# Reordering the start of an adaLN decoder block: evictions placed behind the next casts, the first modulation as wide products, and looser background sums

## The chip, the cores and the metric

The kernel runs on one core of a Trainium2 chip. The metric is the device time of one execution in microseconds, the median over several executions. The engines of the core are named as in the profile: PE multiplies matrices (PEld is its loading of weights), DVE and ACT work on vectors, POOL does a few side jobs here, and SP issues nearly all transfers from the chip's memory. PE writes into eight accumulator banks (PSUM). A bank is usable again when ACT or DVE has copied its content away, which is called an eviction below. Each engine works through its instructions in the order in which they were placed, so an instruction that waits holds up those behind it on the same engine.

## The reference

One decoder layer on 256 tokens of width 2048, all in float32:

```python
mod = jax.nn.silu(c) @ w_ada[l] + b_ada[l]
shift1, scale1, gate1, shift2, scale2, gate2 = jnp.split(mod[:, None, :], N_MOD, axis=-1)
h = rms_norm(x, norm1_gain[l]) * (1 + scale1) + shift1
x = x + gate1 * mixing_sublayer(h, ...)
h = rms_norm(x, norm2_gain[l]) * (1 + scale2) + shift2
x = x + gate2 * swiglu(h, w_ffn_in[l], w_ffn_out[l])
```

The mixing sublayer projects `h` with `w_in` (13 column blocks of 512 for queries, keys and values, then more for gates), runs three branches (stick-breaking attention, dilated window attention, gated linear attention), gates and sums them, and projects with `w_out`. The conditioning vector `c` gives six modulation vectors of 2048 through the matrix `w_ada` of 2048 x 12288, some 100 MB.

## The kernel before, in words

**Products.** All large products are made from three float32r products (`mm3`, lines 180 to 182): the high part of the activations with the high part of the weights, with the low part of the weights, and the low part of the activations with the high part of the weights. Each weight tile of two k-chunks (128 x 1024, 512 KB) is loaded by SP into a `raw` tile (line 161), rounded by ACT into `whi` (line 172, a cast), and DVE subtracts to get `wlo` (line 173). `whi` and `wlo` have four buffers each. The width of 2048 is cut into 16 chunks of 128; the tokens into two halves, so each column block needs two accumulator banks.

**The first chunks** (`first_chunks`). The input projection starts before all of `h` exists. `x` and the rows of `w_ada` for chunk 0 are loaded first. PE sums the squares of `x` (line 553), DVE and ACT make the root (`root_of`), and the modulation of chunk 0 is a sum over 16 row tiles: ten of them as products on PE with one moving column each (line 724, two per row tile), six of them weighted and added on DVE (line 738) and reduced by one more pair of products. `keep_warm` (line 704) puts products without use between them. Then `make_h` gives `h` for chunk 0, and `start_block` multiplies it with 13 column blocks (line 682), each of 6 products, in the order 1, 2, 3, 4, 9, 10, 11, 12, 0, 5, 6, 7, 8. The results are evicted to the tiles `A0` to `A12` (`evict`, line 630), except those of blocks 5 to 8, which stay in the banks until chunks 1 and 2 are added. Blocks 3, 4, 11, 12, 6 and 7 use the four `misc` banks, the others the four `acc` banks, so block 12 takes over the banks of block 4, and block 10 those of block 2. Meanwhile the modulations of chunks 1 and 2 are made on DVE: `columns` and `chunk_macs` call `column_mac` (line 433), a multiply with a running sum over 1024 columns, four per chunk. Inside `first_chunks` the context `in_order` pins PE, ACT and DVE to the order in which the code is written.

**The visits.** Then 26 visits (`proj_block` from the loop over `visits`) add chunks 1 to 10 to the column blocks, a few chunks at a time, while `ada_chunks` makes the modulation of the next chunks. A visit copies `A[b]` back into two banks (line 618), loads and casts its weights, multiplies, and evicts to `A[b]` again (line 630). Visits take the `acc` and the `misc` banks in turn. After the visits, 13 more blocks (`LAST`) finish the projection while the attention begins.

**Background.** The other four modulation segments are made in small steps between products (`tick` calls the generator `background`). `ada_segment_steps` loads half a row of `w_ada` into a ring of tiles, and `mac` issues the DVE sum. 128 such sums are spread over the stretch from 228 us to 948 us.

**Order.** Outside `in_order`, a scheduler places instructions by priority (`prio` raises it) and readiness, from its own estimate of times. `tc.issue_after(ins)` adds an ordering edge behind `ins`, but only for those instructions of the block that run on the engine of `ins`; others get no edge. `state["split"]` is the newest subtraction of line 173 or 234, on DVE. `state["mm"]` is the newest product of line 182, on PE. `state["cast"]` is the newest cast of line 172, on ACT.

**Constants.** The stick-breaking branch needs three small constant tiles that are loaded behind the visits: `k_low` (line 871, cast by ACT at line 872), `k_bias` (line 873, added by DVE at line 952), and `k_dist`.

Of the kernel before, what the change touches and what calls it, by code (L numbers as in the profile page):

```python
# [17 lines left out]
P = 128  # L18
# [68 lines left out]
def trunk(ctx: ExitStack, tc: tile.TileContext, I, out):  # L87
# [408 lines left out]
    ring = {"tags": ("AR0", "AR1"), "n": 0}  # L496
# [7 lines left out]
    def mac():  # L504
        v, seg, j, half, raw, done = macs.pop(0)
        with tc.issue_after(state["split"].ins):
            column_mac(v, seg, j, half, raw)
        if done is not None:
            after.append(done)

    def ada_segment_steps(v, seg, done):


        for j in range(KC):
            for half in range(2):

                while len(macs) >= len(ring["tags"]) - ring.get("spare", len(ring["tags"]) > 3):
                    mac()
                raw = araw([P, HALF])
                with prio(), tc.issue_after(state["loads_after"]) if "loads_after" in state else nullcontext():  # L520
                    load_column(raw, seg, j, half)
# [109 lines left out]

    def first_chunks():
# [9 lines left out]
        def load_two(k, b, single=False):  # L642
            raw = raws[k, b] = wp.tile([P, 2, NB], F32, tag="raw", name=nm("raw"))
# [6 lines left out]
        def load_one(k, b):  # L650
            raw = raws[k, b] = wp.tile([P, 2, NB], F32, tag="raw", name=nm("raw"))
# [32 lines left out]
        def x_in(j, a, b):  # L684
            nc.sync.dma_start(xT[j][:, a:b], I["x_t"][:, 4 * j + a : 4 * j + b, :])

        def mods_in(j, a, b):
            nc.sync.dma_start(rows[j][:, a:b], I["ada_0"][:, 4 * j + a : 4 * j + b, :])

# [6 lines left out]
        for b in (3, 9, 11):  # L696
            load_two(0, b)
        load_mods(1, (0, 1))

# [6 lines left out]
        with in_order():  # L706
            csil = silu_of_c()
            near1 = small([P, 1])
            nc.vector.tensor_scalar(near1, vec[:, BADA + SEG_SCALE1 * KC : BADA + SEG_SCALE1 * KC + 1], 1.0, None, op0=ALU.add)
# [8 lines left out]
            mods = [acc_bank([P, 1]) for _ in range(2)]  # L718
            part = S("T6", [P, 2 * P])

            def by_pe(lhs, k, stop=False):
                for i in range(2):
                    c = slice(i * P, (i + 1) * P)
                    nc.tensor.matmul(
                        mods[i], lhs[:, c], eps_c[:, 2:3] if k is None else csil[:, k : k + 1], start=k == 0, stop=stop
                    )

            def on_pe(*ks):
                for k in ks:
                    by_pe(rows[k // 4][:, k % 4, :], k)  # L730
# [16 lines left out]
            on_dve(2, 3)  # L747
            on_pe(0, 1)
            r = state["root"] = root_of(sums)
            keep_warm(WARM[5])  # L750
            on_pe(4, 5)
            on_dve(6, 7)
# [1019 lines left out]
```

## Time and profile before

| | us |
|---|---|
| median of 3 runs | 1593.93 (1589.18 to 1599.44) |
| the profiled execution, its own time | 1592.44 |
| span in its profile | 1590.7 |
| PE busy in the span | 1560.7 |
| DVE busy | 1372.6 |
| ACT busy | 917.4 |

The profile's page lists busy time per engine, the span in 40 slices, and the costliest groups of instructions. Busy PE is not PE at its peak: products overlap, so the better measure is the number of products in a stretch. A table of stretches gives for each the length, and per engine the busy time with the number of instructions in brackets, then the granted PE clock (1.00 is full), the share of the transfer engines, and GB/s. A line of the timeline gives start, duration, engine, line, operation, output and inputs, count, and in square brackets how long the engine had been idle before and what ended that.

### The profile page before, as it was taken

To read this page: it belongs to the slowest core of one execution; us is meant where nothing else is said; L and a number is where in the kernel's file an instruction comes from. 1 tells how busy PE (TensorE), PEld (TensorE's weight loads), DVE (VectorE), ACT (ScalarE), POOL (GpSimd) and SP (SyncE) were. 2 spreads that over 40 slices of the span, in tenths; PEclk is the share of its full clock that TensorE was granted. 3 is DMA by queue.
4 is the path that set the end of the run, shared out by engine and by line. 5 is a ranking of instruction groups with operands and counts; after the bars stand their busy time and mean duration, and the time that the engine had idled before them with its cause. 6 is when DMAs were issued, how large, how long until landed. Compare 5 with 4: busy or idle time off the path is not lost.

```text
span 1590.7 us, 20098 instructions
## 1 busy us (share of the span) xinstructions
PE 1560.7 (98%) x7082; PEld 1283.0 (81%) x7082; DVE 1372.6 (86%) x1838; ACT 917.4 (58%) x1292; POOL 5.0 (0%) x11
## 2 busy tenths in 40 slices
PE   9999999999999999999998999999999999999998
PEld 8687778788887878888876888888888888888887
DVE  7888877788898999987886878999999999789886
ACT  6786677775765655344434745555655555455553
POOL 0000000000000000000000000000000000000000
PEclk9999999999999999999999999999999999999999
DMA  9998968767777777989898776666566566656664
GB/s 330 399 351 316 349 225 299 242 222 221 242 270 264 261 272 240 309 288 339 305 320 292 264 241 204 194 213 208 186 191 220 185 199 225 199 186 192 231 206 138
DMA packets 113780, 399.20 MB, mean 251 GB/s; under 512 B 12528, under 2 KB 13424, under 8 KB 113680
## 3 DMA queue, kind: packets, MB, share of 16 engines
q1 hardware_dynamic: 113104, 395.84, 73.4%
q0 software_dynamic: 576, 2.10, 0.3%
q8 instruction: 55, 0.90, 0.2%
q14 instruction: 45, 0.37, 0.1%
HBM read 393.69 MB, written 4.19 MB: 250 GB/s over the span
## 4 chain that ended last, share of the span: by engine, by line
PE 58%; DMA 4%; DVE 3%; issue 1%; ACT 1%; SPq 0%; ACTq 0%; DVEq 0%
PE acc L181 12%; PE acc L182 12%; PE acc L180 12%; PE misc L181 7%; PE misc L182 7%; PE misc L180 7%; DMA raw<-w_out 3%; DVE wlo L173 1%; ACT whi L172 1%; PE misc L1407 0%; DMA A<-x_blocks 0%; DMA T<-w_in 0%; DMA KD<-ada_t 0%; DVE wlo L234 0%; PE acc L1407 0%
## 5 line engine op out<-in xcount | busy, mean ns | idle before, releaser
L181 PE MATMUL acc<-wlo,H 128*128 128x512 f32 (+1 forms) x856 | 335.6, 392 | 5.4 <-DVE wlo L173 3.1
L180 PE MATMUL acc<-whi,H 128*128 128x512 f32 (+1 forms) x856 | 333.4, 393 | 4.3 <-ACT whi L172 4.3
L182 PE MATMUL acc<-whi,H 128*128 128x512 f32 (+1 forms) x856 | 334.3, 391 | 0.0
L172 ACT CAST whi<-raw 128x1024 fp32r<-128x1024 f32 x204 | 209.8, 1035 | 202.7 <-PE acc L182 95.4
L173 DVE TENSOR_TENSOR wlo<-raw,whi 128x1024 fp32r<-128x1024 f32 x204 | 242.1, 1197 | 91.8 <-ACT whi L172 91.2
L181 PEld LDWEIGHTS acc<-wlo,H 128*128 128x128 f32 x856 | 161.2, 188 | 42.3 <-DVE wlo L173 7.1
L180 PEld LDWEIGHTS acc<-whi,H 128*128 128x128 f32 x856 | 160.8, 188 | 38.6 <-ACT whi L172 5.6
L182 PEld LDWEIGHTS acc<-whi,H 128*128 128x128 f32 x856 | 161.1, 188 | 32.7 <-DVE H L598 0.2
L248 ACT CAST whi<-raw 128x1024 fp32r<-128x1024 f32 (+1 forms) x133 | 128.1, 977 | 80.1 <-PE acc L182 32.2
L234 DVE TENSOR_TENSOR wlo<-raw,whi 128x1024 fp32r<-128x1024 f32 (+1 forms) x133 | 147.8, 1127 | 17.2 <-ACT whi L248 16.1
L181 PE MATMUL misc<-wlo,H 128*128 128x512 f32 x285 | 111.5, 391 | 1.1 <-DVE wlo L173 1.0
L182 PE MATMUL misc<-whi,H 128*128 128x512 f32 x285 | 110.4, 388 | 0.0
L180 PE MATMUL misc<-whi,H 128*128 128x512 f32 x285 | 108.9, 388 | 1.1 <-ACT whi L172 1.1
L181 PE MATMUL acc<-wlo,A 128*128 128x512 f32 x210 | 82.6, 393 | 4.3 <-DVE wlo L173 4.2
L182 PE MATMUL acc<-whi,A 128*128 128x512 f32 x221 | 86.3, 391 | 0.0
L180 PE MATMUL acc<-whi,A 128*128 128x512 f32 x210 | 82.4, 392 | 2.4 <-ACT whi L172 2.4
L181 PEld LDWEIGHTS misc<-wlo,H 128*128 128x128 f32 x285 | 53.5, 188 | 15.1 <-DVE wlo L173 4.4
L180 PEld LDWEIGHTS misc<-whi,H 128*128 128x128 f32 x285 | 53.4, 188 | 12.5 <-ACT whi L172 1.5
L182 PEld LDWEIGHTS misc<-whi,H 128*128 128x128 f32 x285 | 53.5, 188 | 10.8
L234 DVE TENSOR_TENSOR A<-raw,A 128x1024 fp32r<-128x1024 f32 (+2 forms) x58 | 54.3, 943 | 2.7 <-ACT A L248 2.1
L630 ACT COPY A<-acc 128x512 f32<-128x512 f32 x66 | 37.6, 592 | 28.5 <-PE acc L182 25.6
L433 DVE CUSTOM_DVE_ANT_0 AR<-AR,ada,vec 128x1024 f32<-128x1024 f32 x36 | 46.1, 1279 | 7.9 <-DMA AR<-ada_t 7.9
(725 smaller groups left out, 3265.0 us busy)
## 6 DMA issues: line engine op xcount, KB each, us to landing
raw<-w_in SPq DMA_DIRECT2D x143, 512.0 KB, 5.6
raw<-w_ffn_in SPq DMA_DIRECT2D x137, 512.0 KB, 4.5
raw<-w_ffn_out SPq DMA_DIRECT2D x74, 512.0 KB, 4.4
AR<-ada_t SPq DMA_DIRECT2D x71, 512.0 KB, 5.5
X<-w_in SPq DMA_DIRECT2D x34, 512.0 KB, 5.3
raw<-w_out SPq DMA_DIRECT2D x32, 512.0 KB, 7.4
OS<-ada_t SPq DMA_DIRECT2D x29, 512.0 KB, 7.3
KD<-ada_t SPq DMA_DIRECT2D x22, 512.0 KB, 6.2
```

The lines of the kernel that those rows point to most:

```text
L172: state["cast"] = nc.scalar.copy(hi[:, :n, :], raw[:, :n, :])
L173: state["split"] = nc.vector.tensor_tensor(lo[:, :n, :], raw[:, :n, :], hi[:, :n, :].bitcast(F32), op=ALU.subtract)
L180: nc.tensor.matmul(ps, lh, rh, start=start, stop=False, skip_group_check=seeded)
L181: nc.tensor.matmul(ps, lh, rl, start=False, stop=False, skip_group_check=seeded)
L182: state["mm"] = nc.tensor.matmul(ps, ll, rh, start=False, stop=stop, skip_group_check=seeded)
L234: done = nc.vector.tensor_tensor(dst, x, y, op=ALU.subtract)
L248: nc.scalar.copy(hi[:, :n, :], src)
L433: return nc.vector.tensor_tensor_reduce(out=raw, in0=raw, in1=cB[:, half * HALF : (half + 1) * HALF], scale=1.0, scalar=part if half else ...
L630: nc.scalar.copy(A[b][:, t, :], pss[t])
```

## The change

There are five parts.

1. **Visits.** A new function `visit` replaces `proj_block` in the loop over `visits`. It leaves the finished banks in a list `pending` and evicts up to two of them behind the last cast of the next visit. At the end of `first_chunks` only block 5 is evicted at once; 6, 8 and 7 go into the list.
2. **Chunk 0's modulation.** The stationary operand is now one column of silu(c) repeated 128 times, the moving operand a row tile of 256 columns, so that every partition of one bank holds all 256 sums, and one product per row tile replaces two. DVE picks the diagonal with a multiply-and-sum against the identity (for the scale, the identity times the norm gain). PE takes row tiles 0, 1, 4, 5 and 8 to 13, DVE 2, 3, 6, 7, 14 and 15. Two calls of `keep_warm` go.
3. **Order of the first chunks.** Loads are issued earlier into tiles that are free by then, casts stand one eviction earlier, and `make_h` for chunk 1 stands ahead of the cast of block 7 and the eviction of block 4, where it stood behind the eviction of block 11.
4. **Early constant.** The load of `k_low` gets a raised priority.
5. **Background.** The ring of the first stage has three tiles in place of two, of which one stays spare; `mac` and its load name the newest product in `issue_after` in place of the newest subtraction.

```diff
--- before.py
+++ after.py
@@ -493,7 +493,7 @@
                         make_h(k)
                     yield
 
-    ring = {"tags": ("AR0", "AR1"), "n": 0}
+    ring = {"tags": ("AR0", "AR1", "OD"), "n": 0}
 
     def araw(shape, dtype=F32):
         ring["n"] += 1
@@ -503,7 +503,7 @@
 
     def mac():
         v, seg, j, half, raw, done = macs.pop(0)
-        with tc.issue_after(state["split"].ins):
+        with tc.issue_after(state["mm"].ins):
             column_mac(v, seg, j, half, raw)
         if done is not None:
             after.append(done)
@@ -514,11 +514,12 @@
         for j in range(KC):
             for half in range(2):
 
-                while len(macs) >= len(ring["tags"]) - ring.get("spare", len(ring["tags"]) > 3):
+                while len(macs) >= len(ring["tags"]) - ring.get("spare", len(ring["tags"]) > 2):
                     mac()
                 raw = araw([P, HALF])
-                with prio(), tc.issue_after(state["loads_after"]) if "loads_after" in state else nullcontext():
-                    load_column(raw, seg, j, half)
+                with tc.issue_after(state["loads_after"]) if "loads_after" in state else nullcontext():
+                    with prio(), tc.issue_after(state["mm"].ins):
+                        load_column(raw, seg, j, half)
                 macs.append((v, seg, j, half, raw, done if (j, half) == (KC - 1, 1) else None))
                 yield
 
@@ -629,6 +630,20 @@
             for t in range(NT):
                 nc.scalar.copy(A[b][:, t, :], pss[t])
 
+    pending = []
+
+    def visit(k0, k1, b, bank, carry):
+        pss = [bank([P, NB]) for _ in range(NT)]
+        with prio():
+            for t in range(NT):
+                nc.scalar.copy(pss[t], A[b][:, t, :])
+        w = load_weights(w_in, k0, k1, b)
+        with tc.issue_after(state["cast"].ins):
+            for _ in range(min(2, len(pending))):
+                evict(*pending.pop(0))
+        block(pss, h_at, w_in, k0, k1, b, w=w, go_on=True, more=carry, seeded=True)
+        (carried if carry else pending).append(pss if carry else (b, pss))
+
     def first_chunks():
 
 
@@ -639,16 +654,19 @@
             for i in which:
                 load_column(rows[4 * k + i], (SEG_SCALE1, SEG_SHIFT1)[i // 2], k, i % 2)
 
-        def load_two(k, b, single=False):
-            raw = raws[k, b] = wp.tile([P, 2, NB], F32, tag="raw", name=nm("raw"))
+        def raw_at(tag):
+            return S(tag, [P, 2, NB]) if tag else wp.tile([P, 2, NB], F32, tag="raw", name=nm("raw"))
+
+        def load_two(k, b, single=False, tag=None):
+            raw = raws[k, b] = raw_at(tag)
             for n in range(2) if single else (slice(0, 2),):
                 if single:
                     nc.sync.dma_start(raw[:, n, :], w_in[b + n, :, k, :])
                 else:
                     nc.sync.dma_start(raw, w_in[b : b + 2, :, k, :].rearrange("b p c -> p b c"))
 
-        def load_one(k, b):
-            raw = raws[k, b] = wp.tile([P, 2, NB], F32, tag="raw", name=nm("raw"))
+        def load_one(k, b, tag):
+            raw = raws[k, b] = raw_at(tag)
             nc.sync.dma_start(raw[:, 0, :], w_in[b, :, k, :])
 
         def cast_one(k, b):
@@ -681,21 +699,17 @@
                 for t in range(NT):
                     nc.tensor.matmul(pss[t], h_at(k, t)[l], r, start=start and i == 0, stop=stop and i == 2)
 
...
         nc.sync.dma_start(vec, I["k_vec"])
         for j in range(4):
             nc.sync.dma_start(xT[j], I["x_t"][:, 4 * j : 4 * j + 4, :])
         for j, a, b in ((0, 0, 4), (1, 0, 4), (2, 0, 4), (3, 0, 2), (3, 2, 4)):
             nc.sync.dma_start(rows[j][:, a:b], I["ada_0"][:, 4 * j + a : 4 * j + b, :])
         load_two(0, 1, True)
-        for b in (3, 9, 11):
-            load_two(0, b)
+        load_two(0, 3)
         load_mods(1, (0, 1))
+        load_two(0, 9)
+        load_mods(1, (2, 3))
+        load_two(0, 11)
 
         spare = acc_bank()
 
@@ -705,8 +719,12 @@
 
         with in_order():
             csil = silu_of_c()
-            near1 = small([P, 1])
-            nc.vector.tensor_scalar(near1, vec[:, BADA + SEG_SCALE1 * KC : BADA + SEG_SCALE1 * KC + 1], 1.0, None, op0=ALU.add)
+            gain = vec[:, ROW_N1 : ROW_N1 + 1]
+            o = [BADA + seg * KC for seg in (SEG_SCALE1, SEG_SHIFT1)]
+            near = small([P, 1])
+            nc.vector.scalar_tensor_tensor(near, vec[:, o[0] : o[0] + 1], 1.0, gain, op0=ALU.add, op1=ALU.mult)
+            diag = scr([P, P])
+            nc.vector.tensor_scalar(diag, ident, gain, None, op0=ALU.mult)
             keep_warm(WARM[0])
             turned = spread(csil, [cB[:, q * NB : (q + 1) * NB] for q in range(4)], "KC", True)
             next(turned)
@@ -715,19 +733,15 @@
             for _ in turned:
                 pass
             sums = acc_bank([P, T])
-            mods = [acc_bank([P, 1]) for _ in range(2)]
+            mods = acc_bank([P, 2 * P])
             part = S("T6", [P, 2 * P])
 
-            def by_pe(lhs, k, stop=False):
-                for i in range(2):
-                    c = slice(i * P, (i + 1) * P)
-                    nc.tensor.matmul(
-                        mods[i], lhs[:, c], eps_c[:, 2:3] if k is None else csil[:, k : k + 1], start=k == 0, stop=stop
-                    )
+            def by_pe(lhs, rhs, k, stop=False):
+                nc.tensor.matmul(mods, lhs, rhs, start=k == 0, stop=stop)
 
             def on_pe(*ks):
                 for k in ks:
-                    by_pe(rows[k // 4][:, k % 4, :], k)
+                    by_pe(csil[:, k : k + 1].to_broadcast([P, P]), rows[k // 4][:, k % 4, :], k)
 
             def on_dve(*ks):
                 for k in ks:
@@ -744,27 +758,33 @@
             squares(2, "AR0", sums)
             keep_warm(WARM[4])
             squares(3, "AR1", sums)
-            on_dve(2, 3)
+            on_dve(2, 3, 6, 7)
             on_pe(0, 1)
             r = state["root"] = root_of(sums)
-            keep_warm(WARM[5])
-            on_pe(4, 5)
-            on_dve(6, 7)
-            keep_warm(WARM[6])
-            on_pe(8, 9)
+            on_pe(4, 5, 8, 9, 10, 11)
+            on_dve(14, 15)
+            on_pe(12, 13)
+            by_pe(ones, part, None, True)
             for dst, ps in state["spreads"]:
                 nc.scalar.copy(dst, ps)
-            on_dve(10, 11)
-            on_pe(12, 13)
-            by_pe(part, None)
-            on_pe(14)
-            by_pe(rows[3][:, 3, :], 15, True)
+            load_one(0, 0, "X1")
+            load_two(0, 5, tag="X2")
+            load_two(0, 7, tag="AR0")
+            load_two(1, 5, tag="AR1")
+            load_two(1, 7, tag="KC")
+            rows.extend(S(tag, [P, HALF]) for tag in FIRST_TAGS[:4])
+            load_mods(2, range(4))
+            load_two(2, 5, tag="KD")
+            load_two(2, 7)
             cast_two(0, 1, True)
             lows(0, 1)
-            sh, sc = (mod1[seg][:, 1, 0:1] for seg in (SEG_SHIFT1, SEG_SCALE1))
-            nc.vector.scalar_tensor_tensor(sc, mods[0], near1, vec[:, ROW_N1 : ROW_N1 + 1], op0=ALU.add, op1=ALU.mult)
-            o = BADA + SEG_SHIFT1 * KC
-            nc.vector.tensor_tensor(sh, mods[1], vec[:, o : o + 1], op=ALU.add)
+            for i, seg in enumerate((SEG_SCALE1, SEG_SHIFT1)):
+                col = slice(i * P, (i + 1) * P)
+                nc.vector.tensor_tensor_reduce(
+                    out=part[:, col], in0=mods[:, col], in1=ident if i else diag, scale=1.0,
+                    scalar=vec[:, o[1] : o[1] + 1] if i else near, op0=ALU.mult, op1=ALU.add,
+                    accum_out=mod1[seg][:, 1, 0:1],
+                )
             keep_warm(WARM[7])
             make_h(0, True)
             banks = {}
@@ -782,55 +802,48 @@
                         scaled_gain(mod1[seg], ROW_N1, 1, 2)
 
             lows(0, 1)
-            load_one(0, 0)
-            load_mods(1, (2, 3))
             cast_two(0, 3)
             lows(0, 3)
-            load_two(0, 5)
+            columns(0)
             cast_two(0, 9)
-            lows(0, 9)
-            load_two(0, 7)
-            normed(r, 1, 4)
             start_block(1)
             evict(1, banks[1])
+            lows(0, 9)
+            columns(1)
             cast_two(0, 11)
+            start_block(2)
             lows(0, 11)
-            load_two(1, 5)
-            columns(0, 1)
-            start_block(2)
+            columns(2)
+            cast_one(0, 0)
             evict(2, banks[2])
             start_block(3)
+            lows(0, 0)
+            columns(3)
+            normed(r, 1, 2)
+            cast_two(0, 5)
             evict(3, banks[3])
-            cast_one(0, 0)
-            lows(0, 0)
-            load_two(1, 7)
-            rows.extend(S(tag, [P, HALF]) for tag in FIRST_TAGS[:4])
-            load_mods(2, range(4))
-            columns(2, 3)
             start_block(4)
+            lows(0, 5)
+            make_h(1, True)
+            cast_two(0, 7)
             evict(4, banks[4])
             start_block(9)
+            lows(0, 7)
             evict(9, banks[9])
-            cast_two(0, 5)
-            lows(0, 5)
-            load_two(2, 5)
             start_block(10)
+            cast_two(1, 5)
             evict(10, banks[10])
-            cast_two(0, 7)
-            lows(0, 7)
-            load_two(2, 7)
             start_block(11)
+            lows(1, 5)
+            normed(r, 2, 4)
+            cast_two(1, 7)
             evict(11, banks[11])
-            make_h(1, True)
             start_block(12)
+            lows(1, 7)
             evict(12, banks[12])
-            cast_two(1, 5)
-            lows(1, 5)
             start_block(0)
+            chunk_macs(2, rows[8:12])
             evict(0, banks[0])
-            cast_two(1, 7)
-            lows(1, 7)
-            chunk_macs(2, rows[8:12])
             for k in range(TWO):
                 if k == 2:
                     cast_two(2, 5)
@@ -840,8 +853,8 @@
                     lows(2, 7)
                 for b in BLOCKS_Y:
                     start_block(b, k)
-        for b in BLOCKS_Y:
-            evict(b, banks[b])
+        evict(5, banks[5])
+        pending.extend((b, banks[b]) for b in (6, 8, 7))
 
     with prio(30000):
         first_chunks()
@@ -857,7 +870,8 @@
         steps += 1
     state["load_raws"] = ("X1", "X2", "AR0", "AR1", "KC", "KD")
     for n, (b, k0, k1, until) in enumerate(visits):
-        proj_block(k0, k1, b, carry=n == len(visits) - 1, bank=(acc_bank, misc_bank)[n % 2 if n < len(visits) - 1 else 0])
+        last = n == len(visits) - 1
+        visit(k0, k1, b, acc_bank if last or n % 2 == 0 else misc_bank, last)
         while steps < 4 * (until - TWO):
             next(chunks, None)
             steps += 1
@@ -868,7 +882,8 @@
     kc = S("KC", [P, 8, P])
     low_r, bias = S("T3", [P, P], F32R), kc[:, 1, :]
     low = S("T5", [P, P])
-    nc.sync.dma_start(low, I["k_low"])
+    with prio():
+        nc.sync.dma_start(low, I["k_low"])
     nc.scalar.copy(low_r, low)
     nc.sync.dma_start(bias, I["k_bias"])
     near, far = S("KD", [P, 2, 3 * P]), S("X0", [P, 3 * P])
```

More of the change, by code (lines that the diff above doesn't have):

```diff
@@ L682, in products @@
                     nc.tensor.matmul(pss[t], h_at(k, t)[l], r, start=start and i == 0, stop=stop and i == 2)
[L684 to L688, printed above, removed]
         nc.sync.dma_start(vec, I["k_vec"])
```

## The prediction

> **What bounds the kernel now.** I read the page's busy shares first, then a table of stretches.
>
> ```profile
> PE 1560.7 (98%) x7082; PEld 1283.0 (81%) x7082; DVE 1372.6 (86%) x1838; ACT 917.4 (58%) x1292; POOL 5.0 (0%) x11
> ...
> 20.00:25.00 5.00, 5.00 (x16) 4.15 (x17) 3.95 (x7) 2.75 (x4) 0.00 (x0) 0.58 0.86 314
> 40.00:50.00 10.00, 9.61 (x41) 7.28 (x40) 9.64 (x15) 3.79 (x6) 0.00 (x0) 1.00 1.01 368
> 50.00:60.00 10.00, 8.24 (x34) 5.89 (x33) 9.95 (x16) 10.00 (x19) 0.00 (x0) 1.00 1.03 410
> 60.00:80.00 20.00, 18.41 (x80) 14.28 (x79) 15.75 (x23) 16.66 (x28) 0.00 (x0) 1.00 1.03 410
> 80.00:100.00 20.00, 20.00 (x90) 16.55 (x90) 15.64 (x22) 17.64 (x28) 0.00 (x0) 1.00 0.99 370
> 100.00:120.00 20.00, 19.53 (x87) 15.81 (x86) 17.73 (x25) 16.09 (x26) 0.00 (x0) 1.00 0.93 334
> 120.00:150.00 30.00, 29.50 (x125) 22.67 (x124) 22.69 (x34) 21.64 (x34) 0.00 (x0) 1.00 0.91 332
> 150.00:200.00 50.00, 47.05 (x201) 36.65 (x199) 42.98 (x63) 32.59 (x52) 0.00 (x0) 1.00 0.93 332
> 200.00:205.00 5.00, 2.56 (x11) 1.62 (x10) 2.87 (x3) 5.00 (x8) 0.00 (x0) 1.00 0.39 136
> 291.00:301.00 10.00, 6.24 (x19) 4.92 (x18) 8.72 (x16) 8.65 (x17) 2.08 (x1) 0.66 0.68 221
> 500.00:700.00 200.00, 197.65 (x879) 162.36 (x878) 192.26 (x252) 102.94 (x117) 0.00 (x0) 1.00 0.80 267
> ```
>
> PE is the bound, so what counts is where it falls below its pace. From 80 to 100 us it starts 90 products in 20 us, 0.222 us each. Against that pace 40:50 lacks 4 products (0.9 us), 50:60 lacks 11 products (2.4 us), 60:80 lacks 10 (2.2 us), 100:120 lacks 3 (0.7 us), 120:150 lacks 10 (2.2 us), 150:200 lacks 24 (5.3 us) and 200:205 lacks 11 (2.5 us). The visits from 100 to 205 us thus lose 10.7 us, the stretch from 50 to 80 us 4.6 us. The waits of 46 to 206 us and one place in the timeline say why.
>
> ```profile
> ACT A L630 <- PE misc L182: 15.6, 11, 3.2
> ACT A L630 <- PE acc L182: 14.7, 10, 2.9
> PEld acc L181 <- DVE wlo L173: 6.9, 11, 1.2
> PEld acc L180 <- ACT whi L172: 5.6, 3, 2.3
> ```
> ```profile
> 183.28 1.26 ACT L630 COPY A<-misc 128x512 f32<-128x512 f32 x2 [2.78 <-PE misc L182]
> ...
> 184.44 1.05 ACT L172 CAST whi<-raw 128x1024 fp32r<-128x1024 f32 x1
> ...
> 185.54 0.73 PE L180 MATMUL acc<-whi,H 128*128 128x512 f32 x2 [1.62 <-ACT whi L172]
> ```
>
> ACT stands 2.78 us before the eviction of a visit that PE is still working on; the cast of the next visit's weights is queued behind it, and PE, done at last, waits 1.62 us for that cast. ACT spends 30.3 us so.
>
> **Part 1, evictions behind the next casts.** The added wait is the same (an eviction still waits for PE), but behind it stand now only the seeds and casts of the visit after next, a visit further off. Four `whi` buffers hold two or three tiles of the next visit while this one runs. Visits take the two pools in turn and two banks each, so a bank is needed again four visits later, and an eviction that comes one visit later costs nothing; were that cover gone, each visit would lose one pair of evictions, 1.26 us. What comes late next is DVE: the subtraction follows the cast on a DVE that is 86% busy in 150:200 (42.98 of 50). The losses are 10.7 us; those that end at a cast vanish, those in which DVE was at a sum of the modulation stay in part (the row of waits for `wlo` counts 6.9 us, some of it behind late casts too). I take a gain of 7 us, bounds 3 (only the casts' own 5.6 us, less 2.6 given back to DVE) and 10.7.
>
> In 50:80 the same queue stands at the hand-over, where ACT is full: 10.00 busy of 10. The evictions of blocks 6, 8 and 7 are postponed, not saved, so of 4.6 us I take 3, bounds 0 and 4.6.
>
> **Part 2, chunk 0's modulation.** These rows carry it.
>
> ```profile
> 12.22 1.02 PE L553 MATMUL acc<-AR,ones_r 128*128 128x256 f32 x4
> 16.16 2.04 DVE L738 SCALAR_TENSOR_TENSOR T<-OS,tiny,T 128x256 f32<-128x256 f32 x4
> 18.25 1.01 PE L724 MATMUL acc<-eps_c,T 128*128 128x1 f32 x4 [0.43 <-DVE T L738]
> 19.13 1.85 PE L724 MATMUL acc<-tiny,OD 128*128 128x1 f32 x8
> 20.58 0.22 DVE L765 SCALAR_TENSOR_TENSOR scale<-acc,tiny,vec 128x1 f32<-128x1 f32 x1 [1.78 <-PE acc L724]
> 21.20 0.60 ACT L593 ACTIVATE H<-T,shift,scale 128x256 fp32r<-128x256 f32 x1 [3.57 <-DVE shift L767]
> 22.69 1.78 PE L682 MATMUL acc<-whi,H 128*128 128x512 f32 x4
> 27.93 1.28 DVE L433 CUSTOM_DVE_ANT_0 T<-T,ada,vec 128x1024 f32<-128x1024 f32 x1
> ```
>
> A wide product has the shape of the square sums, two records, at most 0.51 us (1.02 for 4, the tail of the last one with it). Eleven of them from 13.2 us, the reducing one last, end between 18.3 and 18.8; I take 18.5, where the last product now ends near 20.5. DVE is no longer late for it: it adds two tiles after the root instead of four (2.04 us for four, so done at 17.2); the two added before the root fill a gap in which it waits for the square sums, and the two new small steps (0.22 us each by the row of line 765) lie beside the warming products. The pick costs two multiply-and-sums of 128 columns; between 0.22 us for one column and 1.28 for 1024 lies 0.35 each, 0.85 with the reads, against 0.6 for the two small steps now. So the shift is ready at 19.4 in place of 21.2, 1.8 us earlier, and the first product starts near 20.0. The granted clock is 0.58 in 20:25, and the first four products take 0.44 us each; with wide products PE has no thin stretch before, so I take 0.9 us more (four products at 0.222). Sum: 2.7 us; bounds 1.5 (slow clock as now, products at 0.51) and 3.
>
> [...]
>
> **Part 3, the order of the first chunks.** Here the gain is lost again, I think. More rows:
>
> ```profile
> L646 SPq DMA_DIRECT2D raw<-w_in x2: 327/328/328, 6.5 to 8.6; - x2
> ...
> DMA to landing us min/median/max: 7.7/8.4/9.1
> ```
> ```profile
> 32.12 1.09 ACT L630 COPY A<-acc 128x512 f32<-128x512 f32 x2
> 33.08 1.09 ACT L667 CAST whi<-raw 128x1024 fp32r<-128x1024 f32 x1
> 33.83 2.35 DVE L671 TENSOR_TENSOR wlo<-raw,whi 128x1024 fp32r<-128x1024 f32 x2
> 34.02 1.11 ACT L630 COPY A<-misc 128x512 f32<-128x512 f32 x2
> ```
>
> From start to start an eviction pair and a cast take 0.95 us on ACT each, a subtraction 1.17 and a sum 1.32 (1.28 and its read) on DVE. Transfers land in order at about 400 GB/s (410 in 50:60), 1.3 us for 512 KB. Blocks 1 and 2 are in at 16.3 (8.6 plus 7.7). Then come block 3, two rows of chunk 1, block 9, two more rows, block 11: seven pieces, 9.1 us, so block 11's weights are in at 25.4, where today no row of chunk 1 stands ahead of them. ACT's cast of block 11 starts there, then the half cast of block 0 (0.55), and evicts block 2 by 27.9. PE, at six products (1.33 us) a block from 20.0, wants block 2's banks for block 10 at 26.7, gets the first at 27.4 and loses 0.7 us; at block 11 it loses 0.6 for block 3's. Worse, ACT's `make_h` for chunk 1 stands ahead of block 4's eviction and needs all four sums of chunk 1. On DVE these come behind the subtraction of block 11 (26.5 to 27.6): a sum, the half subtraction of block 0, a sum, and the norm's 256 columns, 1.32 + 0.6 + 1.32 + 0.3, so 31.2. Then `make_h` 0.5, cast of block 7 0.95, first copy of block 4 0.5: 33.2. PE stands before block 12 from 30.6 to 33.2, 2.6 us. In all 3.9 us lost against 2.7 gained, but with PE later the 0.9 us in 40:50, a wait for the last sums of chunk 2, go. Parts 2 and 3 together: 0. Bounds: minus 1.5 (2.7 + 0.9 - 3.9, and a slow clock after the stop as in 20:25) and plus 3.6 (no stop at all). The earlier loads themselves cost nothing: they wait on SP for tiles that DVE and ACT have left by then.
>
> **Part 4, the early constant.**
>
> ```profile
> 282.28 0.65 SPq L873 DMA_DIRECT2D KC<-k_bias  x1
> ...
> 287.89 0.30 ACT L872 CAST T<-T 128x128 fp32r<-128x128 f32 x1 [6.21 <-DMA T<-k_low]
> ...
> 290.32 0.75 DVE L952 TENSOR_TENSOR misc<-misc,KC 128x256 f32<-128x256 f32 x2
> ...
> 295.18 0.69 PE L969 MATMUL misc<-T,T 128*128 128x384 f32 x1 [3.76 <-ACT T L960]
> ```
> ```profile
> DMA to landing us min/median/max: 7.1/7.1/7.1
> ```
>
> ACT's 6.21 us wait for `k_low` goes, as SP issues it ahead of weights, which are set back by one issue, 0.65 us at the most (the row of line 873), beside loads that run a visit ahead. PE's 3.76 us and the slow clock behind it (0.66 in 291:301) lack 26 products, 5.8 us. But line 952 needs `k_bias`, issued at 282.28 and landed 7.1 us later (the last row is line 873's), at 289.4. The chain to line 969 can start only 0.9 us earlier; with ACT and DVE free of their backlog it may run shorter by 1 to 2 us. I take 2, bounds 0 and 5.8.
>
> **Part 5, the background.** `mac` is a DVE instruction and its load stands on SP; an edge behind a product on PE reaches neither. So the sums lose the edge they had (behind the newest subtraction) and get none; the third ring tile lets a load go one sum earlier. The stretches behind 300 us are nearly at pace (879 products in 200 us of 900). I take 0, bounds plus and minus 3.
>
> **The sum**: 7 + 3 + 0 + 2 + 0 = 12 us. The profiled execution took 1592.44 us (span 1590.7), so 1580.4; the median of the runs, 1593.93, is 1.5 us above it, so 1582. All low ends (3 + 0 - 1.5 + 0 - 3) lose 1.5 us, all high ends (10.7 + 4.6 + 3.6 + 5.8 + 3) gain 27.7.
>
> **Rivals.** *Full gain* (1.0 of each part): the order in the first chunks does not stop PE, as ACT reaches block 4's eviction in time, and the chain at 291 us runs free. For it: the change's loads leave early; against it: the sums of chunk 1 are fixed in DVE's order. 10.7 + 4.6 + 3.6 + 4 = 23, so 1571. Chance 0.2.
>
> *DVE takes over*: the casts come early, but PE then waits for subtractions behind sums, and part 5 lets more sums in. For it: DVE is 86% busy in 150:200; against: its load does not grow. Then part 1 gives its low ends, 3, and part 4 its 2: 5 us gained, 1589. Chance 0.22.
>
> *Slower*: the freed sums are placed before their rows have landed and hold DVE. Place: 500 to 750 us, where DVE is busy 192.26 of 200, a slack of 4% or 10 us.
>
> ```profile
> DVE AR L433 <- DMA AR<-ada_t: 13.0, 8, 4.3
> ```
>
> This row of the waits of 200 to 900 us gives 1.6 us a wait; of some 44 sums there more than 6 must wait before the slack is used up; half of them cost 35 - 10 = 25 us, so 1607, two thirds 37, so 1619. Against it: only 8 wait today, and the ring gives an earlier load. Chance 0.08, of which 0.05 above 1%.
>
> [...] It lies inside the forecast's case and has 0.05 of its chance.
>
> *Not what it says*: part 5 as above; its time is that of the forecast.
>
> **The numbers.** Forecast 0.5 (1575 to 1588 by itself). A measurement of this kernel tells about 1% from no change, 16 us: faster means below 1578. From the forecast 0.15 lie there, from the full gain all 0.2; slower by 1% 0.05. Range 1568 to 1593: it leaves out the best end of the full gain, the worst of the DVE case and nearly all of the slower one.
>
> **What would show it.** Part 1: line 630 no longer ahead of line 172 at a visit's start, 150:200 with over 215 products. Part 3: PE idle before its eighth block near 31 us, with ACT's line 593 waiting for DVE. Part 4: line 872 without a wait, line 952 waiting for `k_bias`. Wrong would be: waits of line 173 replaced by nothing while 100:205 stays as it is, or long waits of line 433 for its rows.

## The result and the profile after

| | us |
|---|---|
| median of 4 runs | 1620.63 (1619.18 to 1621.63) |
| the kernel before beside it | 1594.92 (1589.18 to 1599.44) |
| ratio after to before | 1.0166, 95% interval 1.0135 to 1.0198 |
| span in its profile | 1619.3 (before 1590.7) |

The kernel is slower by 1.7%, outside the predicted range. Parts 1 to 4 gain about what they should; part 5, which I had costed at nothing, takes 2.2% (its edge put back) to 2.7% (part 5 alone). The table of stretches of the kernel after (length, then busy time and instructions of PE, PEld, DVE, ACT, POOL, then PE clock, share of the transfer engines, GB/s):

```profile
20.00:25.00 5.00, 5.00 (x23) 4.02 (x23) 5.00 (x7) 2.81 (x5) 0.00 (x0) 1.00 1.04 400
25.00:40.00 15.00, 13.09 (x48) 8.27 (x47) 12.80 (x20) 13.71 (x24) 0.00 (x0) 1.00 1.04 397
...
50.00:60.00 10.00, 8.25 (x35) 6.18 (x34) 10.00 (x16) 10.00 (x18) 0.00 (x0) 1.00 1.03 409
...
150.00:200.00 50.00, 49.48 (x218) 40.52 (x217) 46.30 (x68) 37.48 (x58) 0.00 (x0) 1.00 0.84 307
...
340.00:400.00 60.00, 39.74 (x175) 32.67 (x174) 37.29 (x58) 24.98 (x45) 1.26 (x1) 0.80 0.62 214
490.00:550.00 60.00, 41.85 (x197) 32.70 (x196) 46.77 (x110) 42.74 (x87) 0.00 (x0) 0.86 0.43 144
```

The same two late stretches in the kernel before:

```profile
340.00:400.00 60.00, 59.87 (x327) 49.57 (x325) 51.88 (x71) 34.74 (x61) 0.00 (x0) 1.00 0.66 205
490.00:550.00 60.00, 59.25 (x267) 48.29 (x266) 58.13 (x78) 36.74 (x46) 0.00 (x0) 1.00 0.76 254
```

The visits run as hoped: 218 instructions on PE in 150:200 where there were 201. The time is lost in two later stretches, where PE was nearly full before. There it is busy for 40 and 42 us of 60, and its clock falls too (0.80 and 0.86, where it was 1.00).

To see where a lead is won or lost I compare the start of the n-th product of 512 columns, the warming products left out, in both traces (after minus before, at the time before in brackets): -3.0 us (20), +1.0 (40), -1.8 (100), -11.4 (205), -18 (300), -52.6 (400), +29.7 (520), +28.7 (end). So at 400 us the kernel after was far ahead in these dense products, and by 520 us it had given back 82 us. It had not worked faster: it had done dense products that before came later, and put the attention off. Its waits from 340 to 560 us show what stopped it (engine, its tile and line, what it waited for: us in total, times, longest):

```profile
PE misc L984 <- ACT T L975: 19.6, 1, 19.6
DVE AR L433 <- DMA AR<-ada_t: 12.7, 6, 3.7
ACT T L970 <- DVE misc L967: 11.9, 2, 11.3
...
PE misc L1221 <- DVE T L1209: 11.2, 1, 11.2
...
PE misc L940 <- DVE A L928: 4.6, 1, 4.6
```

The places of the attention's constants in time (start, duration, engine, line, operation) tell why. Lines from the visits on stand some 15 higher in the kernel after: line 967 is line 952 before, 970 is 955, 984 is 969.

```profile
196.60 0.33 SPq L886 DMA_DIRECT2D T<-k_low  x1
...
369.04 0.33 SPq L426 DMA_DIRECT2D AR<-ada_t  x1
370.18 0.33 SPq L161 DMA_DIRECT2D raw<-w_in  x1
370.55 0.43 SPq L888 DMA_DIRECT2D KC<-k_bias  x1
```
```profile
367.72 1.29 DVE L433 CUSTOM_DVE_ANT_0 AR<-AR,ada,vec 128x1024 f32<-128x1024 f32 x1 [3.65 <-DMA AR<-ada_t]
...
373.17 1.28 DVE L433 CUSTOM_DVE_ANT_0 AR<-AR,ada,vec 128x1024 f32<-128x1024 f32 x1 [3.02 <-DMA AR<-ada_t]
...
375.95 0.76 DVE L967 TENSOR_TENSOR misc<-misc,KC 128x256 f32<-128x256 f32 x2 [1.49 <-DMA KC<-k_bias]
376.42 0.87 ACT L970 ACTIVATE T<-misc 128x384 f32<-128x384 f32 x2 [11.27 <-DVE misc L967]
...
383.09 0.51 ACT L975 CAST T<-T 128x384 fp32r<-128x384 f32 x1 [2.97 <-POOL KC L896]
...
383.65 0.69 PE L984 MATMUL misc<-T,T 128*128 128x384 f32 x1 [19.59 <-ACT T L975]
```

`k_low` leaves early, as the change says. But `k_bias`, issued at 282.28 before, leaves at 370.55. 63 more transfers than before have been issued on SP ahead of it: 27 rows for the modulation sums and 36 tiles of dense weights. Each row needs a ring tile that DVE frees by a sum, and DVE in turn waits up to 3.65 us for the row of its next sum. ACT, whose next step needs line 967, stands 11.27 us. PE stands 19.59 us before line 984, the next in its order. Behind it in that order stand dense products whose weights are already cast: ACT casts no weights from 365.2 to 399.8 us, and PE goes on with dense products at 390.97. `k_bias` is not the only late constant in this stop: near its end ACT waits 2.97 us for POOL's cast of `k_lvl` (line 896), whose load was issued at 375.34 us. The later stop before line 1221, 11.2 us up to 522.28 us, I read as the debt: the dense products that lay beside these steps before are used up. That before line 940 has another cause, as the second experiment shows.

### The profile page after: what moved, and what is told of

Its sections match the earlier page's. It is cut to its first block, busy times and chain, and to the rows that moved or that the text cites. A ratio compares the mean times of both kernels' runs of the same rounds, so it can differ in the third digit from the quotient of the medians.

```text
span 1619.3 us, 20061 instructions
## 1 busy us (share of the span) xinstructions
PE 1563.5 (97%) x7056; PEld 1283.0 (79%) x7056; DVE 1379.3 (85%) x1842; ACT 932.1 (58%) x1303; POOL 4.2 (0%) x11
## 4 chain that ended last, share of the span: by engine, by line
PE 74%; DMA 9%; DVE 8%; issue 3%; ACT 3%; SPq 0%; POOL 0%; DVEq 0%; ACTq 0%; POOLq 0%
PE acc L181 15%; PE acc L182 15%; PE acc L180 15%; PE misc L181 8%; PE misc L182 8%; PE misc L180 8%; DMA KC<-ada_t 2%; DVE wlo L173 2%; DMA KD<-ada_t 2%; DMA AR<-ada_t 2%; DVE wlo L234 2%; DMA raw<-w_in 1%; DVE A L234 1%; PE misc L1093 1%; PE misc L700 1%
## 5 line engine op out<-in xcount | busy, mean ns | idle before, releaser
L433 DVE CUSTOM_DVE_ANT_0 AR<-AR,ada,vec 128x1024 f32<-128x1024 f32 x32 | 41.0, 1280 | 17.4 <-DMA AR<-ada_t 17.4
L173 DVE TENSOR_TENSOR wlo<-X,whi 128x1024 fp32r<-128x1024 f32 (+1 forms) x36 | 39.2, 1102 | 11.4 <-ACT whi L172 11.3
```

The lines of the kernel that those rows point to most:

```text
L173: state["split"] = nc.vector.tensor_tensor(lo[:, :n, :], raw[:, :n, :], hi[:, :n, :].bitcast(F32), op=ALU.subtract)
L433: return nc.vector.tensor_tensor_reduce(out=raw, in0=raw, in1=cB[:, half * HALF : (half + 1) * HALF], scale=1.0, scalar=part if half else ...
```

## The experiments

Theory A: the swapped edge sets the modulation sums free, and loads with a raised priority (those of the sums and of the weights) are placed ahead of the constants, which carry none; the attention is then placed late and stands without cover. Theory B: the freed sums hold DVE, as in the prediction's rival. Theory C: the third ring tile does it. The kernel before took 1591.92 us beside the first four, 1593.32 beside the next four and 1592.01 beside the last; what counts is the ratio.

**The old edge again**, in the kernel after:

```diff
-        with tc.issue_after(state["mm"].ins):
+        with tc.issue_after(state["split"].ins):
             column_mac(v, seg, j, half, raw)
```

> The changed kernel with one line undone: the background sums stand again behind the newest subtraction (an edge on DVE). Theory A (the freed sums and their loads keep SP busy with transfers of raised priority, so that k_bias and the other constants are placed 64 transfers later and the attention's sums 360 products later on PE): all of the loss goes, the gain up to 280 us (11 us) stays, 1578 to 1586 us. Theory B (the freed sums hold DVE while their rows are on the way): the same, 1578 to 1590. Theory C (the third ring tile is the cause): still near 1620.

Measured: 1582.43 us, ratio 0.9945 (0.9927 to 0.9964). `k_bias` leaves 100 us earlier, and PE's long stop is 1.6 us. Timeline and waits of this kernel:

```profile
270.37 0.42 SPq L888 DMA_DIRECT2D KC<-k_bias  x1
...
276.72 0.76 DVE L967 TENSOR_TENSOR misc<-misc,KC 128x256 f32<-128x256 f32 x2 [4.20 <-DMA KC<-k_bias]
```
```profile
PE misc L984 <- ACT T L975: 1.6, 1, 1.6
```

One line of the change makes 2.2% of the time. The ring keeps its three tiles here, and the loads keep their new edge, so C falls: the third tile by itself does not do it. A and B both expect this result. Whether the freed sums do it with two tiles, no run shows.

**The constants early, the sums still free**, in the kernel after:

```diff
-    nc.sync.dma_start(bias, I["k_bias"])
+    with prio():
+        nc.sync.dma_start(bias, I["k_bias"])
...
+    with prio():
+        nc.sync.dma_start(lvl_f, I["k_lvl"])
```

The loads of `k_dist` and `w_gla_a` get the same.

> The changed kernel with its freed background sums kept, and the raised priority of k_low given to the other constants too (k_bias, k_dist, k_lvl, w_gla_a). Theory A: the late constants were the whole loss, so 1574 to 1586 us, with no wait of some 20 us near 360 us and none of line 1221 near 500 us. Theory B: the freed sums still stand on DVE before their rows, so 1600 or more.

Measured: 1585.69 us, ratio 0.9955 (0.9934 to 0.9976). Timeline, waits of 340 to 560 us and stretches of this kernel:

```profile
197.97 0.39 SPq L889 DMA_DIRECT2D KC<-k_bias  x1
```
```profile
DVE AR L433 <- DMA AR<-ada_t: 12.5, 10, 2.2
...
DVE KC L433 <- DMA KC<-ada_t: 5.8, 4, 2.3
...
PE misc L945 <- DVE A L933: 4.0, 1, 4.0
```
```profile
340.00:400.00 60.00, 59.98 (x321) 49.79 (x320) 52.78 (x76) 36.31 (x84) 0.00 (x0) 1.00 0.71 225
490.00:550.00 60.00, 56.28 (x243) 45.76 (x242) 54.40 (x73) 33.78 (x44) 0.00 (x0) 0.94 0.74 257
```

The sums are as free as in the kernel after, and still most of the loss is gone. DVE's waits for the rows of sums, which B blames, are still there: 18.3 us in these two rows, where the kernel after has 23.2 and the kernel before 4.7. So what cost most of the time is the constants that were pushed back, not the sums and their waits. A holds for most of the loss; it had expected all of it. A smaller loss stays, 56 busy us of 60 in 490:550 behind a wait of 4.0 us. Line 945 here is line 940 of the kernel after, so this stop stays with the free sums, where both repairs leave 1.3 us of it; it is what B can claim. Four constants moved at once, and which of them carries how much is not shown.

**Part 5 alone**, in the kernel before:

```diff
-    ring = {"tags": ("AR0", "AR1"), "n": 0}
+    ring = {"tags": ("AR0", "AR1", "OD"), "n": 0}
...
-        with tc.issue_after(state["split"].ins):
+        with tc.issue_after(state["mm"].ins):
             column_mac(v, seg, j, half, raw)
...
-                with prio(), tc.issue_after(state["loads_after"]) if "loads_after" in state else nullcontext():
-                    load_column(raw, seg, j, half)
+                with tc.issue_after(state["loads_after"]) if "loads_after" in state else nullcontext():
+                    with prio(), tc.issue_after(state["mm"].ins):
+                        load_column(raw, seg, j, half)
```

> The kernel before with part 5 alone (freed sums, third ring tile). Theory A: the constants come late here too, and nothing is gained elsewhere: before plus 32 to 42 us (the 28 to 34 us by which the changed kernel is behind after 520 us, and the 11 us that it had gained by 280 us), 1627 to 1637. Theory B: 1610 to 1640, spread over 300 to 900 us rather than in two stops. If the loss needs the other parts too: near 1595.

Measured: 1635.32 us, ratio 1.027 (1.0223 to 1.0317). Timeline and waits of this kernel:

```profile
384.27 0.43 SPq L873 DMA_DIRECT2D KC<-k_bias  x1
```
```profile
PE misc L969 <- ACT T L960: 21.0, 1, 21.0
PE misc L1206 <- DVE T L1194: 11.1, 1, 11.1
PE misc L925 <- DVE A L913: 5.1, 1, 5.1
```

The same three stops, without any other part of the change: part 5 alone costs 43 us. Here `k_low` leaves late too, at 383.80 us.

**The visits alone**, in the kernel before:

```diff
-        proj_block(k0, k1, b, carry=n == len(visits) - 1, bank=(acc_bank, misc_bank)[n % 2 if n < len(visits) - 1 else 0])
+        last = n == len(visits) - 1
+        visit(k0, k1, b, acc_bank if last or n % 2 == 0 else misc_bank, last)
```

The list `pending`, the function `visit` and the new end of `first_chunks` (only block 5 evicted at once) come with it.

> The kernel before with part 1 alone (evictions of the visits behind the next casts). By the count of products the changed kernel gains 9.6 us between 100 and 205 us. If that is part 1, this kernel takes 1582 to 1587 us; if the reordered start of the kernel has a share in it, 1588 to 1593.

Measured: 1582.08 us, ratio 0.9944 (0.9921 to 0.9966). Stretches and the waits of 46 to 206 us of this kernel:

```profile
100.00:205.00 105.00, 104.47 (x461) 86.07 (x460) 94.95 (x134) 80.50 (x125) 0.00 (x0) 1.00 0.94 352
```
```profile
ACT A L630 <- PE misc L182: 5.8, 5, 1.2
...
PEld acc L181 <- DVE wlo L173: 3.7, 3, 2.2
ACT A L630 <- PE acc L182: 3.2, 6, 1.9
```

ACT's waits before an eviction fall from 30.3 to 9.0 us, and the product count gains 10.1 us by 205 us, of which 0.5 by 100 us.

**The first chunks alone** (parts 2 and 3), in the kernel before:

```diff
-            mods = [acc_bank([P, 1]) for _ in range(2)]
+            mods = acc_bank([P, 2 * P])
...
-                    by_pe(rows[k // 4][:, k % 4, :], k)
+                    by_pe(csil[:, k : k + 1].to_broadcast([P, P]), rows[k // 4][:, k % 4, :], k)
...
+            make_h(1, True)
+            cast_two(0, 7)
             evict(4, banks[4])
```

> The kernel before with parts 2 and 3 alone (chunk 0's modulation as wide products, and the new order and loads of the first chunks; evictions of the visits, the early constant and the background as before). My forecast for these parts was 0 (minus 1.5 to plus 3.6 us of gain). The prediction's theory (what the front gains is lost again in PE's waits for banks) expects PE's product count 3 us ahead of the kernel before at 25 us, 1 us behind it at 40 us, and the time within 2 us of before: 1590 to 1594. The rival (the earlier loads spare the later chunks a wait, so the gain lasts) expects it 2 to 4 us ahead from 60 us on: 1588.

Measured: 1591.56 us, ratio 0.9988 (0.9971 to 1.0005). The product count is 4.0 us ahead at 25 us, 2.7 behind at 40, 0.4 behind at 70. PE's timeline has two stops, before blocks 10 and 12, and the slow clock behind the second (0.50 from 34.17 to 37.59 us, the row is below) takes more:

```profile
27.80 1.45 PE L686 MATMUL acc<-whi,H 128*128 128x512 f32 x4 [1.45 <-ACT A L631]
...
33.31 1.83 PE L686 MATMUL misc<-whi,H 128*128 128x512 f32 x4 [1.67 <-ACT A L631]
```

**The early `k_low` alone**, in the kernel before:

```diff
-    nc.sync.dma_start(low, I["k_low"])
+    with prio():
+        nc.sync.dma_start(low, I["k_low"])
```

> The kernel before with part 4 alone (k_low's load at raised priority). If PE's stop near 291 us (3.76 us before line 969) hung on k_low, the stop goes and the time falls by 4 to 6 us, to 1586 to 1588. If k_bias takes over at once, as I predicted, ACT's wait of 6.2 us at line 872 goes, DVE then waits some 4 to 6 us at line 952 for k_bias, PE's stop shrinks by at most 2 us, and the time is 1590 to 1592.

Measured: 1592.26 us, ratio 0.9987 (0.997 to 1.0004). Timeline of this kernel:

```profile
288.49 0.76 DVE L953 TENSOR_TENSOR misc<-misc,KC 128x256 f32<-128x256 f32 x2 [6.21 <-DMA KC<-k_bias]
...
294.36 0.69 PE L970 MATMUL misc<-T,T 128*128 128x384 f32 x1 [3.55 <-ACT T L961]
```

The wait of 6.21 us has moved, to the hundredth, from `k_low` on ACT to `k_bias` on DVE, and PE's stop is 3.55 us where it was 3.76. The product count is level at 400 us (0.1 us behind) and at 800 (0.9 behind); the lead of 2.6 us that this trace has by 870 us comes from a stretch that the edit does not touch, in which the kernel before has 3.41 us of slow clock (0.50 from 863.86 us). So in these traces the gain is not part 4's.

**Both repairs**: the old edge and the early constants, in the kernel after (the diffs of the first two experiments).

> The kernel after with both repairs: mac's sums are again ordered behind the newest subtraction, and k_bias, k_dist, k_lvl and w_gla_a get k_low's raised priority. With the edge back alone DVE still waited 4.2 us for k_bias at line 967 and PE stood 2 us before line 984 at 280.7 us. If those two stops hang on k_bias, they go and the time is 1.5 to 3 us under the run with the edge back alone (1582): 1579 to 1581. If they hang on DVE's and ACT's backlog, it stays at 1582 within 1 us.

Measured: 1578.01 us, ratio 0.9906 (0.988 to 0.9932), a little better than expected. No wait for a constant is left among PE's waits of 220 to 560 us, of which this is the longest:

```profile
PE misc L945 <- DVE A L933: 1.3, 1, 1.3
```

The change and these three kernels, which hold all of its other parts, make a square:

| ratio to before | constants late | constants early |
|---|---|---|
| sums free | 1.0166 (the change) | 0.9955 |
| sums tied to the subtraction | 0.9945 | 0.9906 |

Early constants are worth 2.1% where the sums are free and 0.4% where they are tied (there the two intervals overlap a little): the free sums do most of their damage through the constants, and 0.5% without them. By the first column the free sums cost 2.2%.

**The first chunks reordered**, with the old edge:

```diff
         load_two(0, 9)
-        load_mods(1, (2, 3))
         load_two(0, 11)
+        load_mods(1, (2, 3))
...
-            make_h(1, True)
             cast_two(0, 7)
...
             evict(10, banks[10])
+            make_h(1, True)
```

> The kernel after with mac's old edge, and two edits in the first chunks: block 11's weights are loaded ahead of rows 2 and 3 of chunk 1, and make_h for chunk 1 stands behind the eviction of block 10 in place of ahead of the cast of block 7. If PE's stops from 26 to 38 us come from those two orders, as I predicted, they (about 4.5 us together) go, no stop over 0.5 us is left from 23 to 40 us, and the time is 3 to 4 us under the run with the edge back alone (1582): 1578 to 1579. If ACT's load is what stops PE (casts and evictions take 0.95 us each, and 50 to 60 us is full), half of it comes back by 60 us: 1580 to 1581.

Measured: 1579.72 us, ratio 0.9925 (0.9902 to 0.9949); beside the old edge alone, 0.9945, that is not told apart, and the time lies between the two expectations. The stop before block 12 is gone, but that before block 10 stayed and had another owner. Timeline of this kernel:

```profile
26.64 0.62 ACT L675 CAST whi<-X 128x512 fp32r<-128x512 f32 x1 [2.34 <-DMA X<-w_in]
27.16 1.07 ACT L631 COPY A<-acc 128x512 f32<-128x512 f32 x2
...
27.80 1.45 PE L700 MATMUL acc<-whi,H 128*128 128x512 f32 x4 [1.80 <-ACT A L631]
```

Now ACT is done early with block 11 and stands 2.34 us before block 0's weights, which are needed far later, with block 2's eviction queued behind: the pattern of the visits again.

**Both repairs and that queue undone**: as in the last two, and block 0's cast behind the evictions of blocks 2 and 3, the later casts one or two evictions later:

```diff
-            cast_one(0, 0)
             evict(2, banks[2])
             start_block(3)
+            evict(3, banks[3])
+            cast_one(0, 0)
             lows(0, 0)
...
+            start_block(4)
+            evict(4, banks[4])
             cast_two(0, 5)
-            evict(3, banks[3])
-            start_block(4)
...
+            start_block(10)
+            evict(10, banks[10])
             make_h(1, True)
-            cast_two(0, 7)
-            evict(4, banks[4])
...
             cast_two(1, 5)
-            evict(10, banks[10])
```

> The kernel with the old edge and all small constants early (1578.0, ratio 0.9906), and the first chunks in another order: block 11's weights ahead of rows 2 and 3 of chunk 1, the cast of block 0 behind the evictions of blocks 2 and 3 in place of ahead of them, make_h for chunk 1 behind the eviction of block 10. In the last run ACT stood 2.34 us for block 0's weights (landed at 26.6) with block 2's eviction queued behind, and PE stopped 1.8 us for that at 25.6. If this queue is what stops PE, nothing over 0.5 us is left between 23 and 35 us, PE's product count at 40 us is 2 to 3 us ahead of the kernel before (now 0.5 to 2 behind), and the time is 2 to 3 us less: 1575 to 1576. If PE's stops between 50 and 60 us take it back (ACT is busy all the time there, whatever the order ahead), the lead at 70 us is that of now, 0.4 to 1.6 us, and the time stays at 1578.

Measured: 1575.24 us, ratio 0.9886 (0.9859 to 0.9913), the shortest of all kernels here, with both repairs and this order 1.1% under the kernel before and 2.8% under the change. PE's timeline of this kernel has one stop left from 20 to 40 us, before block 6; I had expected none over 0.5 us up to 35:

```profile
34.88 1.45 PE L700 MATMUL misc<-whi,H 128*128 128x512 f32 x4 [1.45 <-ACT A L631]
```

The product count leads by 4.3 us at 30, 1.8 at 40 and 4.3 at 70 us, where both repairs alone lead by 0.4 at 70; the profiles' spans differ by 2.5 us (1573.3 and 1575.8). But 0.4 is the low end for that order: the three other kernels whose first chunks stand as in the change lead by 0.8 to 1.9 at 70 us (the change 1.8), as loads land at other times (ACT waits 1.90 us for block 11's weights in the change and 3.15 with both repairs). So the step gains 2.4 to 3.9 us in single traces; the two ratios' intervals overlap, and the times do not show it.

## Why the prediction failed

**Part 5 is the step that failed.** The prediction said: the sums "lose the edge they had (behind the newest subtraction) and get none", and took "0, bounds plus and minus 3". The first half was right. The price was not: I sought it where the sums run ("the stretches behind 300 us are nearly at pace") and in whether DVE has room, as in the rival from 500 to 750 us. It lay in what the freed work is placed ahead of. Part 5 alone costs 2.7%, 43 us, and for the most part through loads on SP: `k_bias` 102 us later, PE's stops of 21.0, 11.1 and 5.1 us. For part 4 the prediction had asked what its load sets back on SP (the weights, "by one issue"); for part 5 it did not ask. How the scheduler came to move 36 weight tiles ahead along with 27 rows is not shown. The rival of slower time had its sign right, and its waits, which the prediction named as a sign of being wrong, came: DVE stands 63.5 us from 228 to 960 us before sums whose rows have not landed, 13.4 in the kernel before. But with the constants early 44.0 us of them stay, and that kernel is faster than before. So the place and the price were wrong, and that 1619, its price with two thirds of the waits, lies near the time is chance.

**Part 1 was right, its size only as a sum**: forecast 7 us for 100 to 205 and 3 for the hand-over. Alone it gives 0.56%, 8.9 us. By the product count nearly all of it, 9.6 us, comes from the visits and only 0.5 from the hand-over: there ACT is full (10.00 of 10 in 50:60 after, as before), so postponed evictions only move the queue. DVE took nothing over: the waits for `wlo` in the banks `acc`, 6.9 us before, are 3.7.

**Parts 2 and 3 were right as a sum, not as a list.** Forecast 0, alone 0.12% (the interval spans none). The gain was forecast as 2.7 us, at most 3. In the kernel after the first dense product starts at 19.71 us, 3.0 us earlier than before (22.69), and at 25 us the lead is 3.6. The working did not agree with itself: the sum has 1.8 for the start and 0.9 for the clock, but from 22.69 to its "near 20.0" is 2.7 for the start alone. The 0.9 was an estimate from the clock of 0.58 in 20:25; in the kernel after it is 1.00 there. The loss, forecast as 3.9, is 4.6 us from 25 to 40 us. Both are larger, by 0.9 and 0.7 us, and that this cancels is luck. And of the stops before blocks 10, 11 and 12, put at 0.7, 0.6 and 2.6 us, the trace has these:

```profile
26.73 0.62 ACT L675 CAST whi<-X 128x512 fp32r<-128x512 f32 x1 [0.88 <-DMA X<-w_in]
...
27.89 1.45 PE L700 MATMUL acc<-whi,H 128*128 128x512 f32 x4 [1.06 <-ACT A L631]
...
32.57 1.48 PE L700 MATMUL misc<-whi,H 128*128 128x512 f32 x4 [0.84 <-ACT A L631]
```

These are the stops before blocks 10 and 12. PE's idle time in 25:40 is 1.9 us; the rest of the loss lies in the groups of four themselves, which take 1.45 us and more behind a late eviction, against 1.09 for the one at 21.21 us that waits for none. I blamed block 11's load and `make_h`; the first stop hangs on block 0's load too, which I had given to ACT as 0.55 us of work without asking when its weights land. Only the last experiment, which moves that cast, removes it.

**Part 4 was right in its mechanism, and its size is luck**: `k_bias` takes over the wait, as forecast. But PE's stop shrank by only 0.2 us, less than the 0.9 of the working, and the product count shows no gain there. That the time alone fell by 0.13%, 2.1 us, beside a forecast of 2 is chance, and the interval spans none. In the whole change the part is buried: `k_bias` sets the time there, 88 us later than before.

The sum of parts 1 to 4, 12 us, stands beside 8.8 us (0.55%, 5.7 to 11.6) with the old edge and 15 (0.94%) with the constants early too; most of it is part 1's.

## What to carry to other kernels

Ask of an ordering edge what it holds back, not only what it makes wait: when it goes, work with a raised priority can pass what has none (here 63 transfers passed `k_bias`), and the price appears wherever a small, late load now stands behind it. A product count against time shows a lead that is only work taken from later: the 52.6 us here were a debt, and the stretch that lost its cover paid it. A wait at the head of an in-order queue is removed by taking the waiting step out of the queue's way (the eviction in the visits, block 0's cast here), and whoever does it should ask when each step's own input lands.

## What the runs showed of the hardware

In the kernel with both repairs the clock fell from 1.00 to 0.50 behind a single stop of 2.48 us:

```profile
28.27 1.78 PE L700 MATMUL acc<-whi,H 128*128 128x512 f32 x4 [2.48 <-ACT A L631]
```

With the first chunks alone it fell to 0.50 behind stops of 1.45 and 1.67 us, 5.5 us apart. Single stops of 1.80 us (the first reordering) and 1.45 us (the last kernel) left it at 1.00 throughout 20 to 40 us.

So in these four traces the length of a stop does not settle it alone. These are the 3.41 us up to the fall and the slow stretch behind it, of the kernel with both repairs and of the first chunks alone, and 3.41 us with the stop in the last kernel:

```profile
25.79:29.20 3.41, 0.93 (x4) 0.58 (x4) 1.95 (x2) 3.03 (x5) 0.00 (x0) 1.00 1.06 388
29.20:32.61 3.41, 3.41 (x10) 2.64 (x9) 3.41 (x7) 2.18 (x5) 0.00 (x0) 0.50 1.04 402
```
```profile
30.76:34.17 3.41, 1.74 (x7) 0.89 (x6) 3.31 (x7) 2.93 (x6) 0.00 (x0) 1.00 1.03 411
34.17:37.59 3.42, 3.42 (x10) 2.66 (x9) 1.45 (x3) 2.57 (x5) 0.00 (x0) 0.50 1.03 390
```
```profile
33.08:36.49 3.41, 1.97 (x8) 1.13 (x7) 3.09 (x5) 3.41 (x7) 0.00 (x0) 1.00 1.02 402
```

Up to the fall PE is busy for 0.93 and for 1.74 us of 3.41; in the 3.41 us with the stop that left the clock at 1.00 it is busy for 1.97 us. How long a stop must be, or how little PE must do, for the clock to fall is not shown. The slow stretches differ in length: in the kernel before the clock is 0.50 for 6.83 us from 17.35 us, for 6.82 from 293.83 and for 3.41 from 863.86, in the kernel after for 23.89 us from 366.18 us.

At 17.35 us in the kernel before, no stop of PE lies just ahead of the fall: PE counts as busy throughout the 3.41 us up to it (13.94 to 17.35 us), mostly with one-column products. In the kernel after and with the first chunks alone, where these products are wide, the clock is 1.00 from 20 to 25 us, against 0.58 before.
